# Four-ahead splits in an order that every engine keeps, and the loop over further blocks ahead of the experts

## The chip, the cores and the metric

The kernel runs on one core of a Trainium2 chip. The metric is the device time of one execution, in microseconds, as the median of several runs. Beside it there is one profiled execution with its own time; its span, from the first to the last instruction, is a little shorter than its time.

## What is computed

Two blocks of a sequence model stand one behind the other, on 1024 tokens of width 1024, all in fp32. The first has a gated convolution, a gated linear recurrence and a feed-forward layer, the second a state-space mixer, an mLSTM mixer and a mixture of experts. The change touches the mixture alone: 32 experts in 4 groups, each token goes to the two best experts of its best group.

```python
def hier_moe(h, wg, bg, we, be, w_gate, w_up, w_down):
    ...
    ids = (g_sel * EXPERTS_PER_GROUP + top_i).reshape(-1).astype(jnp.int32)
    order = jnp.argsort(ids)
    tok = order // TOP_K
    xs = xf[tok]
    sizes = jnp.bincount(ids, length=N_EXPERTS).astype(jnp.int32)
    hg = lax.ragged_dot(xs, w_gate.astype(xs.dtype), sizes)
    hu = lax.ragged_dot(xs, w_up.astype(xs.dtype), sizes)
    ys = lax.ragged_dot(jax.nn.silu(hg) * hu, w_down.astype(xs.dtype), sizes)
    ys = ys * gates.reshape(-1)[order][:, None].astype(ys.dtype)
    y = jax.ops.segment_sum(ys, tok, num_segments=t)
```

An expert's gate and up weights are 1024 x 512, its down weights 512 x 1024. 2048 rows are shared out over 32 experts, 64 on average.

## The kernel before, in words

The kernel has stages. `stage1`, `stage2` and `stage4` compute the first block, the mixers and, in `route` (L1462), the routing in two halves of 512 tokens. `stage5` (L1625) computes the experts, adds their two results to each token and normalises.

**Products.** Every fp32 product is made of three matmuls on a faster 32-bit type. `split` (L51) makes two tiles out of weights: ScalarE copies the high half (L56), VectorE, or GpSimd where `low` says so, subtracts it from the weights for the low half (L57). `mm3` (L84) issues high x high, high x low and low x high (L87 to L89). A pair of halves is a *unit*: 128 x 1024 weights, from a pool of five buffers. A unit feeds six matmuls of 128 x 512. `to_T` (L129) turns rows to columns on TensorE, four transposes per PSUM tile (L135), with a high half by ScalarE (L138) and a low half by VectorE out of PSUM (L139).

**The routing.** `route` computes each token's experts and its place within them, and makes with matmuls (L1589) the table `slots`: for the first 128 places of each expert the row of the result, the token and the gate. `sidx` (L1597) holds the first two as integers. Each half also scatters 16-byte records into a list in DRAM (`scatter`, 8 DMAs of GpSimd, L1611), which only the loop over further blocks reads. `cum` counts tokens per expert (L1593).

**The experts.** An expert has 12 units: four of the gate, four of up, four of down. The tokens of an expert are gathered by GpSimd's DMA into one of two tiles `xg` (L1654), transposed and split (`prep`), multiplied by gate and up (`wide`), `th = (tanh(gate/2) + 1) * gate` (L1713, L1714) and `th * up` (L1718), transposed and split again (`hidT`), multiplied by down (`down`), scaled by the gate (L1694) and scattered to `yd` (L1695). The Python loop runs expert e's gate, then the hidden transposes of e - 1, then expert e's up, the token transposes of e + 1 and the down of e - 1. Weights come as 1 MB tiles, two units each, on SP's queue, into 14 buffers (`rawt`).

What stands in the program is not the order on the engines: the framework's scheduler chooses, per engine, which ready instruction comes next, by its own estimate of times. Every sixth low half in the order of the calls is GpSimd's.

**Further blocks.** An expert with more than 128 tokens needs further blocks of 128. After e = 16 `overflow` (L1743) counts tokens with a matmul, makes a table of blocks `ti` with small jobs on VectorE (L1755 to L1773), loads the number of blocks into a register of every engine (L1774), and runs a loop with as many turns (L1776). With this data it has none: no instruction of its body is in the trace. Behind the loop a new block of the program begins.

Of the kernel before, what the change touches and what calls it, by code (L numbers as in the profile page):

```python
# [8 lines left out]
F32 = mybir.dt.float32  # L9
# [7 lines left out]
P = 128  # L17
S = 1024
# [13 lines left out]
class Net:  # L32
# [1429 lines left out]
    def route(self, hf, src, wk, small, wide, mx):  # L1462
# [106 lines left out]
        qs = []  # L1569
        for s, gt in ((0, pg), (1, m2)):  # L1570
# [21 lines left out]
        for tt in range(4):  # L1592
            v.tensor_tensor(self.cum, self.cum, OC[:, tt], ALU.add)  # L1593
# [29 lines left out]


    def stage5(self):  # L1625
        tc, nc, a = self.tc, self.nc, self.a
        self.wctx.close()
        with ExitStack() as ctx:
# [20 lines left out]
            def split(src, shape):  # L1649
                return self.split(src, shape, low=nc.gpsimd if self.nsplit % 6 == 5 else None)  # L1650

            def gather(e):
                x = xg[e % 2]
                nc.gpsimd.indirect_dma_start(  # L1654
                    out=x, out_offset=None, in_=self.h2d,
                    in_offset=bass.IndirectOffsetOnAxis(ap=self.sidx[:, 1, e:e + 1], axis=0),
                    bounds_check=S - 1, oob_is_err=False)

            def prep(e):
                xT = wk.tile([P, 2, KD, P], F32R, tag="xT5", name="xT5")  # L1660
                self.to_T(psa, xg[e % 2], (xT[:, 0], xT[:, 1]), 0)
                return xT

            def wide(w, e, xT):
                ps = psa.tile([P, DE], F32, tag="gu", name="gu", bufs=4)
                for k in range(0, KD, 4):
                    raw = self.rawt([P, 4, DE])
                    nc.sync.dma_start(raw, w[e, k * P:(k + 4) * P, :].rearrange("(k p) c -> p k c", p=P))
                    for j in range(0, 4, 2):
                        u = split(raw[:, j:j + 2], [2, DE])  # L1670
                        for i in range(2):
                            kk = k + j + i
                            self.mm3(ps, (xT[:, 0, kk], xT[:, 1, kk]), (u[0][:, i], u[1][:, i]), kk == 0, kk == KD - 1)
                return ps

            def hidT(hid):
                hT = wk.tile([P, 2, 4, P], F32R, tag="hT5", name="hT5")
                self.to_T(psa, hid, (hT[:, 0], hT[:, 1]), 0, nk=4)
                return hT

            def down(e, hT):
                pd = [psa.tile([P, 512], F32, tag="dn", name="dn") for _ in range(2)]
                for k in range(0, 4, 2):
                    raw = self.rawt([P, 2, D])
                    nc.sync.dma_start(raw, wd[e, k * P:(k + 2) * P, :].rearrange("(k p) c -> p k c", p=P))
                    for j in range(2):
                        u = split(raw[:, j], [D])
                        for ch in range(2):
                            s = slice(ch * 512, (ch + 1) * 512)
                            self.mm3(pd[ch], (hT[:, 0, k + j], hT[:, 1, k + j]), (u[0][:, s], u[1][:, s]), k + j == 0, k + j == 3)  # L1690
                y = wk.tile([P, D], F32, tag="y5", name="y5")
                gt = self.slots[:, 2, e:e + 1]
                for ch in range(2):
                    nc.scalar.activation(y[:, ch * 512:(ch + 1) * 512], pd[ch], AF.Copy, scale=gt)  # L1694
                i = nc.gpsimd.indirect_dma_start(  # L1695
                    out=self.yd, out_offset=bass.IndirectOffsetOnAxis(ap=self.sidx[:, 0, e:e + 1], axis=0),
                    in_=y, in_offset=None, bounds_check=2 * S - 1, oob_is_err=False)
                for o in self.ysc:
                    tc.declare_no_dep(i.ins, o.ins, reason="different rows")
                self.ysc.append(i)  # L1700

            self.ysc = []
            gather(0)
            gather(1)
            xT = prep(0)
            prev = None
            for e in range(NX + 1):
                if e < NX:
                    if e + 2 < NX:
                        gather(e + 2)  # L1710
                    pg = wide(wg, e, xT)
                    th = wk.tile([P, DE], F32, tag="th5", name="th5")
                    nc.scalar.activation(th, pg, AF.Tanh, scale=0.5)  # L1713
                    nc.vector.scalar_tensor_tensor(th, th, 1.0, pg, op0=ALU.add, op1=ALU.mult)  # L1714
                hT = hidT(prev) if e else None
                if e < NX:
                    pu = wide(wu, e, xT)
                    nc.vector.tensor_tensor(th, th, pu, ALU.mult)  # L1718
                    nxt = prep(e + 1) if e + 1 < NX else None
                if e:  # L1720
                    down(e - 1, hT)
                if e == 2:
                    self.scatter()
                if e == NX // 2:

                    self.overflow(mid, wk, psa, xg[(e + 1) % 2])
                prev, xT = th, nxt
# [15 lines left out]
    def overflow(self, mid, wk, psa, x):  # L1743
# [157 lines left out]
```

## Time and profile before

| | us |
|---|---|
| median of 3 runs | 3355.78 (3353.23 to 3355.95) |
| the profiled execution's own time | 3356.34 |
| its span | 3354.6 |
| TensorE matmuls busy | 3178.5 (95%) |
| TensorE weight loads busy | 2608.5 (78%) |
| VectorE busy | 2221.8 (66%) |
| ScalarE busy | 1520.8 (45%) |
| GpSimd busy | 825.0 (25%) |

The shares are means over all stages. The experts run from about 2680 to 3303 us, and in them the shares are others; so the profile is read there, by windows and by each engine's instructions in order of time. A matmul's duration reaches over the start of the next one; what counts is the distance from start to start. In a row of the timeline the number in brackets is the time the engine was idle just before, and what ended it.

### The profile page before, as it was taken

What the parts mean: (1) busy time and instruction counts of PE and PEld (TensorE: products, weight loads), DVE (VectorE), ACT (ScalarE), POOL (GpSimd) and SP (SyncE); (2) the same over time, 40 slices, a digit from 0 to 9 for tenths busy, and PEclk for the clock granted to TensorE, in tenths of its full rate; (3) what the DMA queues carried; (4) which work ended last, traced back from release to release, by engine and by line L of the source; (5) the groups of instructions that cost most, each with busy time, mean ns of one, the idle gap of its engine ahead of it and who ended that gap; (6) DMA issues with size and microseconds to landing.
All of it is one profiled execution on the core that took longest, in us unless ns stands there. A gap on an engine that the chain in (4) does not pass through costs nothing. (4 is left out here: it accounts for less than half of the span.)

```text
span 3354.6 us, 39834 instructions
## 1 busy us (share of the span) xinstructions
PE 3178.5 (95%) x15193; PEld 2608.5 (78%) x15193; DVE 2221.8 (66%) x2928; ACT 1520.8 (45%) x2069; POOL 825.0 (25%) x758
## 2 busy tenths in 40 slices
PE   8999999999999999999999999899999799989993
PEld 6887888877878888788777888777888677777772
DVE  5437545356475555455796656877657699999986
ACT  3327433246242222344443333433343278878773
POOL 0002210001253443000132111132112244434433
PEclk9999999999999999999999999999999899999997
DMA  4322444323422222555522323333332799969994
GB/s 156 100 89 91 142 155 145 126 92 113 169 76 91 76 79 91 199 193 202 159 88 88 107 82 102 96 116 109 121 101 83 265 340 371 370 241 391 374 357 162
DMA packets 347645, 546.04 MB, mean 163 GB/s; under 512 B 30320, under 2 KB 213116, under 8 KB 345660
## 3 DMA queue, kind: packets, MB, share of 16 engines
q1 hardware_dynamic: 307932, 470.01, 40.8%
q0 software_dynamic: 18640, 48.82, 4.0%
q10 hardware_dynamic: 20880, 24.65, 2.1%
q8 instruction: 120, 1.97, 0.2%
q14 instruction: 73, 0.60, 0.1%
HBM read 506.02 MB, written 54.17 MB: 167 GB/s over the span
## 5 line engine op out<-in xcount | busy, mean ns | idle before, releaser
L57 DVE TENSOR_TENSOR unit<-raw,unit 128x1024 fp32r<-128x1024 f32 x726 | 989.9, 1384 | 490.2 <-ACT unit L56 486.3
L56 ACT ACTIVATE unit<-raw 128x1024 fp32r<-128x1024 f32 (+1 forms) x790 | 813.7, 1045 | 749.9 <-PE acc L89 524.7
L87 PE MATMUL acc<-xT,unit 128*128 128x512 f32 x1360 | 542.8, 400 | 0.6 <-ACT xT L138 0.6
L88 PE MATMUL acc<-xT,unit 128*128 128x512 f32 x1360 | 536.0, 394 | 0.0
L89 PE MATMUL acc<-xT,unit 128*128 128x512 f32 x1360 | 534.3, 393 | 0.0
L87 PEld LDWEIGHTS acc<-xT,unit 128*128 128x128 f32 x1360 | 257.9, 190 | 55.1 <-issue 1.0
L88 PEld LDWEIGHTS acc<-xT,unit 128*128 128x128 f32 x1360 | 257.5, 189 | 54.3 <-issue 3.3
L89 PEld LDWEIGHTS acc<-xT,unit 128*128 128x128 f32 x1360 | 257.3, 189 | 54.0 <-issue 1.0
L57 POOL TENSOR_TENSOR unit<-raw,unit 128x1024 fp32r<-128x1024 f32 x64 | 176.5, 2758 | 273.6 <-issue 221.0
L88 PE MATMUL gu<-unit,xT 128*128 128x512 f32 x512 | 208.4, 407 | 17.4 <-DVE unit L57 12.4
L87 PE MATMUL gu<-unit,xT 128*128 128x512 f32 x512 | 206.1, 402 | 0.8 <-ACT xT L138 0.8
L89 PE MATMUL gu<-unit,xT 128*128 128x512 f32 x512 | 203.3, 397 | 0.1
L88 PE MATMUL acc<-unit,xT 128*128 128x256 f32 (+1 forms) x640 | 196.8, 307 | 2.0 <-DVE unit L57 2.0
L87 PE MATMUL acc<-unit,xT 128*128 128x256 f32 (+1 forms) x640 | 194.3, 309 | 2.6 <-ACT xb L1065 2.5
L89 PE MATMUL acc<-unit,xT 128*128 128x256 f32 (+1 forms) x640 | 196.0, 306 | 0.0
L88 PEld LDWEIGHTS gu<-unit,xT 128*128 128x128 f32 x512 | 96.9, 189 | 55.2 <-DVE unit L57 27.3
L87 PE MATMUL acc<-unit,hid 128*128 128x512 f32 x352 | 137.6, 391 | 0.0
L89 PE MATMUL acc<-unit,hid 128*128 128x512 f32 x352 | 137.2, 390 | 0.0
L88 PE MATMUL acc<-unit,hid 128*128 128x512 f32 x352 | 137.2, 390 | 0.0
L87 PEld LDWEIGHTS acc<-unit,xT 128*128 128x128 f32 x640 | 122.1, 191 | 11.1 <-ACT xb L1065 4.7
L642 PE MATMUL acc<-xe,unit 128*128 128x512 f32 x504 | 123.7, 396 | 5.9 <-DVE u L644 5.9
L88 PEld LDWEIGHTS acc<-unit,xT 128*128 128x128 f32 x640 | 122.3, 191 | 8.2 <-DVE unit L57 2.5
(485 smaller groups left out, 6332.3 us busy)
## 6 DMA issues: line engine op xcount, KB each, us to landing
raw<-in_w_in_dram SPq DMA_DIRECT2D x104, 1024.0 KB, 5.1
raw<-in_exp_w_gate_dram SPq DMA_DIRECT2D x64, 1024.0 KB, 9.6
raw<-in_exp_w_up_dram SPq DMA_DIRECT2D x64, 1024.0 KB, 9.6
raw<-in_exp_w_down_dram SPq DMA_DIRECT2D x64, 1024.0 KB, 10.1
raw<-in_w_ffn_down_dram SPq DMA_DIRECT2D x33, 1024.0 KB, 5.1
raw<-in_w_ffn_gate_dram SPq DMA_DIRECT2D x11, 1024.0 KB, 5.8
raw<-in_w_ffn_up_dram SPq DMA_DIRECT2D x11, 1024.0 KB, 5.1
hidD<-th ACTq DMA_DIRECT2D x44, 256.0 KB, 3.7
```

The source lines that it names most:

```text
L56: nc.scalar.activation(h, src, AF.Copy)
L57: (low or nc.vector).tensor_tensor(l, src, h.bitcast(F32), ALU.subtract)
L87: mm(out, w[0], x[0], start=first, stop=False)
L88: mm(out, w[0], x[1], start=False, stop=False)
L89: mm(out, w[1], x[0], start=False, stop=last)
L642: nc.tensor.matmul(ps, w[i], v[j], start=False, stop=(k == 3 and i == 1), skip_group_check=True)
```

## The change

The routing's second half makes the table of blocks (`blocks`), from the counts, ahead of the list of slots. `stage5` issues the loads of the first 16 units, memsets and the first two gathers, then the loop over further blocks. The list's second scatter has moved into the loop's body. Behind the loop the experts are one stream of units: gate, up of e, down of e - 1. While unit n is multiplied, unit n + 4 is split and the load for n + 16 is issued. GpSimd has the low half of a gate's and a down's first unit. Work of VectorE that follows a product stands one unit later (`later`). `in_order` ties each instruction of TensorE, ScalarE, VectorE and GpSimd behind the loop to the one ahead of it in the program, so that the scheduler has no choice there.

```diff
+        if hf:
+            for tt in range(4):
+                v.tensor_tensor(self.cum, self.cum, OC[:, tt], ALU.add)
+            self.blocks(wk, mx, ones)
         for s, gt in ((0, pg), (1, m2)):
...
+    def in_order(self, begin):
+        last = {}
+        for i in self.nc.cur_bb.bb.instructions[begin:]:
+            if i.engine not in (mybir.EngineType.PE, mybir.EngineType.Activation, mybir.EngineType.DVE, mybir.EngineType.Pool):
+                continue
+            if i.engine in last:
+                self.tc.add_manual_dep(
+                    i, last[i.engine].name,
+                    mybir.DependencyInfo(mybir.DependencyClass.NoSync, mybir.DependencyReason.DATA), reason="order")
+            last[i.engine] = i
...
-            def split(src, shape):
-                return self.split(src, shape, low=nc.gpsimd if self.nsplit % 6 == 5 else None)
...
+            stream = []
+            for e in range(NX + 1):
+                if e < NX:
+                    stream += [(e, 0, i) for i in range(4)] + [(e, 1, i) for i in range(4)]
+                if e:
+                    stream += [(e - 1, 2, i) for i in range(4)]
...
+            def split(n):
+                e, m, i = stream[n]
...
+                units[n] = self.split(src, [2, DE] if m < 2 else [D], low=nc.gpsimd if i == 0 and m != 1 else None)
+            AHEAD = 16
+            for n in range(AHEAD):
+                load(n)
             gather(0)
             gather(1)
...
+            self.overflow(wk, psa, mid.tile([P, D], F32, tag="gB", name="xo"))
+            self.nraw = AHEAD // 2
+            begin = len(nc.cur_bb.bb.instructions)
+            LEAD = 4
...
+            for n in range(LEAD):
+                split(n)
+            xT = x_T(0)
...
+            for n, (e, m, i) in enumerate(stream):
+                if n + AHEAD < len(stream):
+                    load(n + AHEAD)
+                if n + LEAD < len(stream):
+                    split(n + LEAD)
...
+                if m < 2:
+                    for k in range(2):
+                        kk = 2 * i + k
+                        self.mm3(pu if m else pg, (xT[:, 0, kk], xT[:, 1, kk]), (u[0][:, k], u[1][:, k]), kk == 0, kk == KD - 1)
...
+                for f in later.pop(n, ()):
+                    f()
+                if i < 3:
+                    continue
+                if m == 0:
                     nc.scalar.activation(th, pg, AF.Tanh, scale=0.5)
+                    if e:
+                        hT = wk.tile([P, 2, 4, P], F32R, tag="hT5", name="hT5")
+                        ps = tr(hid, 4, 0)
+                        high(hT, ps, 0)
+                    def one(th=th, pg=pg, hT=hT, ps=ps, e=e):
+                        nc.vector.scalar_tensor_tensor(th, th, 1.0, pg, op0=ALU.add, op1=ALU.mult)
+                        if e:
+                            low(hT, ps, 0)
+                    later[n + 1] = [one]
+                elif m == 1:
+                    hid = th
...
+                        for q in (0, 4):
+                            ps = tr(xg[(e + 1) % 2], KD, q)
+                            high(xT, ps, q)
+                            two.append((ps, q))
+                    def one(th=th, pu=pu, xT=xT, two=two):
+                        nc.vector.tensor_tensor(th, th, pu, ALU.mult)
+                        for ps, q in two:
+                            low(xT, ps, q)
+                    if 0 < e < NX - 1:
+                        later[n + 1] = [one]
+                    else:
+                        one()
...
+            self.in_order(begin)
...
         with tc.For_i(0, nb) as i:
+            self.scatter()
+            nc.gpsimd.memset(x, 0.0)
```

How it moves instructions is shown at three places. The first is VectorE in the middle of the experts. L57 is a low half of weights, `xT` and `hT` the low halves of tokens and of the hidden layer, `th` the products out of PSUM. Before:

```order
L1714 SCALAR_TENSOR_TENSOR th_20385<-th_20385,gu 128x512
L139 TENSOR_TENSOR hT_20388<-tp,hT_20388 128x512
L57 TENSOR_TENSOR unit<-raw,unit 128x1024 x3
L1718 TENSOR_TENSOR th_20385<-th_20385,gu 128x512
L57 TENSOR_TENSOR unit<-raw,unit 128x1024
L139 TENSOR_TENSOR xT_20438<-tp,xT_20438 128x512 x2
L57 TENSOR_TENSOR unit<-raw,unit 128x1024 x6
L1714 SCALAR_TENSOR_TENSOR th_20545<-th_20545,gu 128x512
```

Now, with L1780 for the first product, L1796 for the second and L1726 for the low halves out of PSUM:

```order
L1780 SCALAR_TENSOR_TENSOR th_20447<-th_20447,gu 128x512
L1726 TENSOR_TENSOR hT_20487<-tp,hT_20487 128x512
L57 TENSOR_TENSOR unit<-raw,unit 128x1024 x3
L1796 TENSOR_TENSOR th_20447<-th_20447,gu 128x512
L1726 TENSOR_TENSOR xT_20537<-tp,xT_20537 128x512 x2
L57 TENSOR_TENSOR unit<-raw,unit 128x1024 x7
L1780 SCALAR_TENSOR_TENSOR th_20607<-th_20607,gu 128x512
```

Of the seven low halves from the second product to the next expert's first one, one stood ahead of the tokens' low halves; now all seven stand behind them, and VectorE's three jobs out of PSUM follow each other. The second place is GpSimd in the same stretch: weights' low halves, gathers of tokens (`xg`) and scatters of results (`yd`). Before:

```order
L1654 DMA xg_19725<-h2d,sidx 128x1024
L57 TENSOR_TENSOR unit<-raw,unit 128x1024
L1695 DMA yd<-y_20167,sidx 2048x1024
L57 TENSOR_TENSOR unit<-raw,unit 128x1024
L1654 DMA xg_19724<-h2d,sidx 128x1024
L57 TENSOR_TENSOR unit<-raw,unit 128x1024
L1695 DMA yd<-y_20335,sidx 2048x1024
L57 TENSOR_TENSOR unit<-raw,unit 128x1024
```

Now:

```order
L57 TENSOR_TENSOR unit<-raw,unit 128x1024 x2
L1667 DMA xg_19749<-h2d,sidx 128x1024
L1810 DMA yd<-y_20435,sidx 2048x1024
L57 TENSOR_TENSOR unit<-raw,unit 128x1024 x2
L1667 DMA xg_19748<-h2d,sidx 128x1024
L1810 DMA yd<-y_20595,sidx 2048x1024
```

Before, a gather or a scatter stands between any two low halves; now the two low halves of an expert stand together, and gather and scatter behind them. The third place is GpSimd from the routing's end to the first expert. Before:

```order
L1611 DMA lst<-rec,row 32768x4
L1647 MEMSET xg_19724 128x1024
L1647 MEMSET xg_19725 128x1024
L1654 DMA xg_19724<-h2d,sidx 128x1024
L1654 DMA xg_19725<-h2d,sidx 128x1024
L1611 DMA lst<-rec,row 32768x4 x5
L1654 DMA xg_19724<-h2d,sidx 128x1024
L1611 DMA lst<-rec,row 32768x4 x2
L1750 MEMSET ov_22422 128x128
L1761 IOTA ov_i 128x16
L107 DMA gB<-in_norm_f_w_dram 128x1024
L57 TENSOR_TENSOR unit<-raw,unit 128x1024 x2
```

Now, from the last row of the loop's body, the branch back (L1875), on:

```order
L1875 UNCONDITIONAL_BRANCH
L1664 MEMSET xg_19748 128x1024
L1664 MEMSET xg_19749 128x1024
L1667 DMA xg_19748<-h2d,sidx 128x1024
L1667 DMA xg_19749<-h2d,sidx 128x1024
L57 TENSOR_TENSOR unit<-raw,unit 128x1024
L107 DMA gB<-in_norm_f_w_dram 128x1024
L1667 DMA xg_19748<-h2d,sidx 128x1024
L57 TENSOR_TENSOR unit<-raw,unit 128x1024
```

The list's eight scatters (`lst`) are gone from here, and the memsets and the first two gathers stand behind the loop, though the program's text has them ahead of it.

## Rows read from the trace of the kernel before

**Rows 1.** Windows: length; PE, PEld, DVE, ACT, POOL busy us; clock, DMA share, GB/s.

```profile
2720.00:2940.00 220.00, 215.04 (x988) 171.96 (x987) 215.92 (x178) 181.24 (x211) 97.62 (x47) 1.00 1.02 369
3020.00:3060.00 40.00, 39.16 (x180) 31.33 (x179) 39.24 (x33) 32.64 (x39) 18.56 (x9) 1.00 1.04 395
```

**Rows 2.** Timeline of ScalarE, Tanh and high half: start us, us, instruction, [idle].

```profile
2686.21 0.60 ACT L1713 ACTIVATE th<-gu 128x512 f32<-128x512 f32 x1 [0.34 <-PE gu L89]
2703.42 0.60 ACT L1713 ACTIVATE th<-gu 128x512 f32<-128x512 f32 x1 [0.34 <-PE gu L89]
2871.69 0.60 ACT L1713 ACTIVATE th<-gu 128x512 f32<-128x512 f32 x1 [0.34 <-PE gu L89]
2874.92 1.06 ACT L56 ACTIVATE unit<-raw 128x1024 fp32r<-128x1024 f32 x1 [0.25 <-PE gu L89]
2890.47 0.60 ACT L1713 ACTIVATE th<-gu 128x512 f32<-128x512 f32 x1 [0.33 <-PE gu L89]
3013.50 0.59 ACT L1713 ACTIVATE th<-gu 128x512 f32<-128x512 f32 x1
3031.59 0.60 ACT L1713 ACTIVATE th<-gu 128x512 f32<-128x512 f32 x1 [0.34 <-PE gu L89]
3242.90 0.60 ACT L1713 ACTIVATE th<-gu 128x512 f32<-128x512 f32 x1 [2.00 <-PE gu L89]
3283.33 0.60 ACT L1713 ACTIVATE th<-gu 128x512 f32<-128x512 f32 x1 [2.40 <-PE gu L89]
```

**Rows 3.** Timeline of TensorE, a steady expert: the wait, the token transposes.

```profile
2868.01 0.40 PE L87 MATMUL gu<-unit,xT 128*128 128x512 f32 x1
2868.82 0.50 PE L88 MATMUL gu<-unit,xT 128*128 128x512 f32 x1 [0.41 <-DVE unit L57]
...
2877.52 1.03 PE L135 MATMUL tp<-ident,xg 128*128 128x128 f32 x8
2878.31 0.48 PE L87 MATMUL dn<-unit,hT 128*128 128x512 f32 x1
```

**Rows 4.** Timeline of VectorE and GpSimd, one of the last experts.

```profile
3224.00 3.50 DVE L57 TENSOR_TENSOR unit<-raw,unit 128x1024 fp32r<-128x1024 f32 x3 [0.26 <-ACT unit L56]
3228.14 0.69 DVE L1718 TENSOR_TENSOR th<-th,gu 128x512 f32<-128x512 f32 x1 [0.65 <-PE gu L89]
...
3226.94 2.82 POOL L57 TENSOR_TENSOR unit<-raw,unit 128x1024 fp32r<-128x1024 f32 x1 [4.07 <-issue]
```

**Rows 5.** Timeline of GpSimd and VectorE, a steady expert.

```profile
2856.02 3.10 POOL L57 TENSOR_TENSOR unit<-raw,unit 128x1024 fp32r<-128x1024 f32 x1 [5.15 <-issue]
2865.21 2.47 POOL L57 TENSOR_TENSOR unit<-raw,unit 128x1024 fp32r<-128x1024 f32 x1 [4.11 <-issue]
...
2857.23 4.11 DVE L57 TENSOR_TENSOR unit<-raw,unit 128x1024 fp32r<-128x1024 f32 x2 [0.37 <-ACT unit L56]
2864.19 9.11 DVE L57 TENSOR_TENSOR unit<-raw,unit 128x1024 fp32r<-128x1024 f32 x6
```

**Rows 6.** Timeline of VectorE, GpSimd and TensorE at the start of the experts.

```profile
2670.14 0.26 DVE L1594 TENSOR_TENSOR slots<-slots,mx 128x96 f32<-128x96 f32 x1 [2.55 <-PE mx L1589]
...
2668.81 1.86 POOL L1647 MEMSET xg<- 128x1024 f32 x2
2671.53 1.17 POOL L1654 DMA_INDIRECT xg<-h2d,sidx  x1 [0.85 <-POOL xg L1647]
...
2687.43 2.39 POOL L57 TENSOR_TENSOR unit<-raw,unit 128x1024 fp32r<-128x1024 f32 x1
...
2677.46 1.97 PE L135 MATMUL tp<-ident,xg 128*128 128x128 f32 x8 [7.36 <-DMA xg<-h2d,sidx]
```

**Rows 7.** Timeline of VectorE and GpSimd at the loop over further blocks.

```profile
2997.02 0.19 DVE L1755 COPY ov_n<-cnt 128x32 f32<-128x32 f32 x1 [2.40 <-PE cnt L1752]
3002.47 0.18 DVE L1772 CAST ov_t<-ov_f 128x32 int32<-128x32 f32 x1
...
3004.46 1.03 POOL L1654 DMA_INDIRECT xg<-h2d,sidx  x1 [5.61 <-issue]
```

More of the change, by code (lines that the diff above doesn't have):

```diff
@@ L1591, in route @@
                 n += 1
-        for tt in range(4):
-            v.tensor_tensor(self.cum, self.cum, OC[:, tt], ALU.add)
+        if not hf:
+            for tt in range(4):
+                v.tensor_tensor(self.cum, self.cum, OC[:, tt], ALU.add)
         v.tensor_tensor(self.slots, self.slots, pl[:, 0:3 * NX].rearrange("p (j e) -> p j e", e=NX), ALU.add)
@@ L1657, in gather @@
                     bounds_check=S - 1, oob_is_err=False)
[L1659 to L1666, printed above, removed]
-                    raw = self.rawt([P, 4, DE])
[L1668 to L1683, printed above, removed]
-                    raw = self.rawt([P, 2, D])
[L1685 to L1700, printed above, removed]
@@ L1703, in stage5 @@
+            def split(n):
+                e, m, i = stream[n]
+                raw = rawd[e, m, i // 2 * 2]
+                src = raw[:, i % 2 * 2:i % 2 * 2 + 2] if m < 2 else raw[:, i % 2]
+                units[n] = self.split(src, [2, DE] if m < 2 else [D], low=nc.gpsimd if i == 0 and m != 1 else None)
+            AHEAD = 16
+            for n in range(AHEAD):
+                load(n)
             gather(0)
             gather(1)
[L1705 to L1708, printed above, removed]
+            self.ysc = []
@@ new lines, in stage5, with tr, high @@
+            self.overflow(wk, psa, mid.tile([P, D], F32, tag="gB", name="xo"))
+            self.nraw = AHEAD // 2
+            begin = len(nc.cur_bb.bb.instructions)
+            LEAD = 4
+            later = {}
+            def tr(xn, nk, k0):
+                ps = psa.tile([P, 4, P], F32, tag="tp", name="tp")
+                for j in range(4):
+                    nc.tensor.transpose(ps[:, j], xn[:, (k0 + j) * P:(k0 + j + 1) * P], self.ident)
+                return ps
+            def high(dst, ps, k0):
+                nc.scalar.activation(dst[:, 0, k0:k0 + 4], ps, AF.Copy)
@@ L1709, in stage5 @@
+            for n, (e, m, i) in enumerate(stream):
[3 more added lines that the diff above has]
+                    split(n + LEAD)
+                u = units.pop(n)
+                todo = []
+                if m == 0 and i == 0:
                     if e + 2 < NX:
                         gather(e + 2)
-                    pg = wide(wg, e, xT)
+                    pg = psa.tile([P, DE], F32, tag="gu", name="gu", bufs=4)
@@ L1722, in stage5 @@
[L1722 to L1727, printed above, removed]
+                elif m == 1 and i == 0:
+                    pu = psa.tile([P, DE], F32, tag="gu", name="gu", bufs=4)
+                elif m == 2 and i == 0:
+                    pd = [psa.tile([P, 512], F32, tag="dn", name="dn") for _ in range(2)]
+                    if e == NX - 1:
+                        hT = wk.tile([P, 2, 4, P], F32R, tag="hT5", name="hT5")
+                        ps = tr(hid, 4, 0)
+                        high(hT, ps, 0)
+                        low(hT, ps, 0)
@@ new lines, in stage5 @@
+                if m < 2:
+                    for k in range(2):
+                        kk = 2 * i + k
+                        self.mm3(pu if m else pg, (xT[:, 0, kk], xT[:, 1, kk]), (u[0][:, k], u[1][:, k]), kk == 0, kk == KD - 1)
+                else:
+                    for ch in range(2):
+                        s = slice(ch * 512, (ch + 1) * 512)
+                        self.mm3(pd[ch], (hT[:, 0, i], hT[:, 1, i]), (u[0][:, s], u[1][:, s]), i == 0, i == 3)
+                for f in later.pop(n, ()):
+                    f()
```

95 lines of the change are left out of this document (64 added, 31 removed).

## The prediction, written before the changed kernel had run

> **What bounds the kernel now.** Begin with the windows [rows 1]. In the 220 us of the first row VectorE is busy 215.9, TensorE's matmuls 215.0, ScalarE 181.2, GpSimd 97.6: two engines look full. The Tanh of each expert comes once per expert, so the starts of two of them give the period: 2890.47 - 2871.69 = 18.78 us [rows 2]. The same view has one period of 18.09 (3013.50 to 3031.59), just after the loop over further blocks, when VectorE had no backlog; and over the last two experts it has (3283.33 - 3242.90) / 2 = 20.2. The 31 periods from 2686.21 to 3283.33 are the place where this change acts; what stands before the routing keeps its order.
>
> Who waits in a period of 18.78? TensorE, once: a matmul starts 0.81 us after the one ahead of it, 0.41 of it idle for a low half of VectorE [rows 3]. Take the 18.09 for TensorE without waits: eight transposes and their restart are 0.9 (2877.52 to 2878.31 and 0.1), four of them 0.4, which leaves (18.1 - 1.3) / 72 = 0.233 from matmul to matmul. The wait is then 0.81 - 0.23 = 0.58 and a slower restart 0.1, and 18.1 + 0.7 = 18.8 closes the account: TensorE alone would take 18.1 per expert. So VectorE sets the 18.78. Of a period it is busy 215.9 / 220 x 18.78 = 18.4 us. Ten low halves, at 1.15 (three take 3.50), and five half-sized jobs out of PSUM, at up to 0.69 [rows 4], are 14.4 of these. The other 4.0 are in [rows 5]: six halves take 9.11 instead of 6.9, two take 4.11 instead of 2.3, each time across one low half on GpSimd (2.47 and 3.10 us, at 2865.21 and 2856.02). A job of VectorE with both operands in SBUF stands while GpSimd's runs; 2.2 and 1.8 are lost, and 0.37 is idle just ahead of the second.
>
> A job that reads PSUM does not stand. In [rows 4] GpSimd works from 3226.94 for 2.82 us, and in the middle of it VectorE's product with the up projection takes its plain 0.69. All depends on what VectorE has to do while GpSimd splits.
>
> **The change, part by part.** *Order.* Low halves on GpSimd stay two per expert, but are now those of a gate's and a down's first unit, and the order is fixed. I walk one expert, with zero where the gate's last matmul is issued. A unit is six matmuls, 1.40. TensorE: four transposes 0.4, up to 6.0, eight transposes 0.9, down 6.9 to 12.5, next gate 12.5 to 18.1. ScalarE, whose high halves (1.06, [rows 2]) take a unit's buffer when TensorE leaves it: Tanh and hidden high half to 1.3, high half of down's first unit to 2.3; after down's start that of the next gate's first unit to 8.8. GpSimd therefore splits from 2.3 to 4.7 and from 8.8 to 11.2. VectorE: gate product and hidden low half 1.2 to 2.6, both from PSUM, then blocked until 4.7; three halves to 8.1; up product and two token low halves (PSUM) to 9.9 (0.6 each, back to back), blocked until 11.2; seven halves to 19.5, which is 1.4 into the next expert, where it began at 1.2. It does not fall further behind, because the next block ends at 4.7 again. TensorE needs the tightest of these (next gate's first unit, 11.2) at 12.7 and the second (12.3) at 14.1: margins of 1.5 and 1.8. So TensorE never waits, and its 18.1 is the period. From the second Tanh (2703.42) to the last (3283.33) now pass 579.9 us; 30 x 18.1 = 543.0. **-36.9.** The stop for the loop in the middle and the slow last experts are inside this.
>
> The Trainium skill would read [rows 1] otherwise: its page "Perfetto Trace Analysis", section "Identifying the Most-Contended Engine", takes VectorE's occupancy as a fair measure of how full it is, and TensorE's by weight loads. By that VectorE, 98% busy, stays the bound, since it loses no job here, and the sum would be that of the first rival. But by [rows 5], 4 us of that occupancy are standing.
>
> *First experts.* From the first Tanh to the second is 17.21. TensorE waits there for a GpSimd half that starts only at 2687.43 [rows 6], behind the eight list scatters, which now run only inside the loop body and, with no further block, never. Eight units are 11.2, eight transposes 0.8 (2877.52 to 2878.31, [rows 3]) and 0.1 of restart; the first gate of the second expert has no down ahead to hide its token halves, 0.9. Together 13.0. **-4.2.**
>
> *Start.* It pays. (1) The table's VectorE jobs took 5.6 us (2997.02 to 3002.65, [rows 7]); of the 19 now, 12 stand ahead of the gather index, by their share 3.6 us, and between routing jobs, whose latency they fill, they cost less. Bounds 0 (VectorE idles there 2.55 us for TensorE's matmuls, [rows 6]) and 3.6; I take 1.9, about half, since those ahead of these matmuls delay them and those behind fill the wait. The index, 0.3 behind the first row of [rows 6], comes at 2672.3 instead of 2670.4. (2) The other seven are 2.1 us by their share, with two routing jobs and the index 2.6: 2674.9. (3) All engines read the count and branch: GpSimd went on at 3004.46, 1.8 after the last table entry (3002.47 + 0.18): 2676.7. (4) The two memsets and gathers, ahead of the branch in the text, stand behind it in GpSimd's order: memsets 1.86, 0.3, and from gather to the first transpose 5.93 (2671.53 to 2677.46): 2684.8 instead of 2677.46. **+7.3**, between +3 and +11. First units are split meanwhile: four high halves and GpSimd's 2.4 behind two gathers end about when the tokens have been transposed. Eight loads are issued ahead of the branch, six more at once behind it; the eight cover sixteen units, over 22 us.
>
> *At nothing:* the twelve last units behind the last Tanh (as many as before), the final norm (order unchanged), and the loads: per expert 369 GB/s x 18.78 = 6.93 MB, over 18.1 us 383 GB/s, and 395 were moved from 3020 to 3060 [rows 1]. Should the transfers stay at 369, each expert is 0.7 us short, 21 us or seven tiles over all, of fourteen buffers.
>
> Sum: -36.9 - 4.2 + 7.3 = -33.8. The profiled execution took 3356.34 (its span 3354.6 and 1.7 around), 0.6 above the median of 3355.78. 3356.3 - 33.8 - 0.6 = 3322; I say **3322**.
>
> **Rivals.** *VectorE stays the bound* (GpSimd's halves slip to where VectorE splits too): the period stays 18.78, 30 x 0.68 = 20.4 more, **3342**. For it: the standing of [rows 5], and any lag that shifts the pairs. Against: the walk returns to itself, and it would have to lag by over 1.5. Chance 0.15.
>
> *Slower: four units are too short a lead.* ScalarE now cannot pass a Tanh or PSUM copy that waits for TensorE, and GpSimd's half hangs behind it. If the next gate's first low half ends over 1.5 us later than in the walk, TensorE stops in every expert. Its price in the trace is what order alone did to the last experts, 20.2: 30 x 2.1 = 63 more, **3385**. It turns slower than before at a period of 18.1 + 33.8 / 30 = 19.2. For it: 20.2 was seen with no lack of work; GpSimd's half has taken 3.10. Against: even that leaves 0.8. Chance 0.09.
>
> *It does half of what it says:* the stop in the middle goes, but the period stays 18.78 as in the first rival, the first experts do not gain their 4.2, since their halves queue as before, and the start is at its bound, 3.7 more: 20.4 + 4.2 + 3.7 = 28.3 more, **3350**, within 0.2%. For it: the first gather now waits for the branch, and its pieces come from another place of the program. Against: the list scatters are out of GpSimd's way in any case. Chance 0.07.
>
> **How the numbers follow.** Forecast 0.69: 3322, with +-5 from the start and +-6 from 0.2 us of period: 3311 to 3333. The range 3311 to 3344 takes in the first rival. A measurement of this kernel tells 0.2%, 6.7 us. Faster, under 3349: forecast and first rival, 0.84. Same, the third: 0.07. Slower, over 3362.5, the second: 0.09.
>
> **What would show it.** Tanh to Tanh 18.1, without a gap in the middle and at the end; TensorE without waits for low halves; GpSimd's halves beside VectorE's PSUM jobs; VectorE's busy share below 98%; first token transposes near 2685; no list scatter after the routing's first half. Wrong if the period stays at 18.8 with VectorE full (first rival), if TensorE waits for GpSimd in each expert (second), or if ScalarE waits for weights.

## The result: 0.87% faster, and the profile after

The changed kernel took 3326.43 us (median of 4 runs, 3324.03 to 3327.16), the kernel before beside it 3355.86 (4 runs, 3353.23 to 3356.15): a ratio of 0.9913, 95% interval 0.9901 to 0.9925. 3322 was forecast, the range was 3311 to 3344. The profiled execution took 3324.03, its span went from 3354.6 to 3322.3 us.

First the windows of the changed kernel, with the columns of [rows 1]:

```profile
2720.00:2940.00 220.00, 220.00 (x1021) 179.25 (x1020) 209.21 (x183) 187.38 (x221) 101.57 (x50) 1.00 1.02 379
3020.00:3060.00 40.00, 40.00 (x190) 32.71 (x189) 38.20 (x34) 33.46 (x41) 16.92 (x9) 1.00 1.03 378
3060.00:3220.00 160.00, 160.00 (x741) 130.29 (x740) 151.91 (x133) 136.25 (x160) 74.53 (x36) 1.00 1.01 368
```

In these windows TensorE is busy in every microsecond; VectorE has gone from 98% to 95%. Next its Tanhs on ScalarE's timeline, which answer to [rows 2]:

```profile
2693.74 0.60 ACT L1773 ACTIVATE th<-gu 128x512 f32<-128x512 f32 x1 [0.34 <-PE gu L89]
2707.83 0.60 ACT L1773 ACTIVATE th<-gu 128x512 f32<-128x512 f32 x1 [0.34 <-PE gu L89]
...
2870.86 0.60 ACT L1773 ACTIVATE th<-gu 128x512 f32<-128x512 f32 x1 [0.34 <-PE gu L89]
2888.98 0.60 ACT L1773 ACTIVATE th<-gu 128x512 f32<-128x512 f32 x1 [0.34 <-PE gu L89]
...
3251.24 0.60 ACT L1773 ACTIVATE th<-gu 128x512 f32<-128x512 f32 x1 [0.34 <-PE gu L89]
```

The first is 7.5 us later than before. From the first to the second are 14.09 us, and the 30 periods behind them are 18.11 or 18.12 each, with no stop in the middle and no slow end: 543.41 us instead of 579.9. From the last Tanh to the end of the span are 71.06 us, before 71.27.

One steady expert on the timelines of VectorE and GpSimd, which answer to [rows 5]:

```profile
2871.70 0.68 DVE L1780 SCALAR_TENSOR_TENSOR th<-th,gu 128x512 f32<-128x512 f32 x1
2872.30 0.68 DVE L1726 TENSOR_TENSOR hT<-tp,hT 128x512 fp32r<-128x512 f32 x1
2873.88 4.92 DVE L57 TENSOR_TENSOR unit<-raw,unit 128x1024 fp32r<-128x1024 f32 x3 [0.90 <-ACT unit L56]
2878.72 0.68 DVE L1796 TENSOR_TENSOR th<-th,gu 128x512 f32<-128x512 f32 x1
2879.32 1.27 DVE L1726 TENSOR_TENSOR xT<-tp,xT 128x512 fp32r<-128x512 f32 x2
2880.52 9.37 DVE L57 TENSOR_TENSOR unit<-raw,unit 128x1024 fp32r<-128x1024 f32 x7
...
2873.04 2.40 POOL L57 TENSOR_TENSOR unit<-raw,unit 128x1024 fp32r<-128x1024 f32 x1 [5.04 <-ACT unit L56]
2879.44 2.43 POOL L57 TENSOR_TENSOR unit<-raw,unit 128x1024 fp32r<-128x1024 f32 x1 [4.00 <-ACT unit L56]
```

The tokens' two low halves, out of PSUM, run beside GpSimd's second half and keep their 0.6 us each (1.27 for both); the product and the hidden low half end just before its first half begins, the second product just before its second. Each of GpSimd's halves outlasts these jobs: three halves of VectorE take 4.92 instead of 3.50 ([rows 4]), seven take 9.37 instead of about 8.1. So VectorE still stands (is busy without getting on) for 2.7 us per expert instead of 4.0.

The start, on the timelines of VectorE, GpSimd and TensorE, which answers to [rows 6]:

```profile
2670.96 0.18 DVE L1602 TENSOR_SCALAR sidx<-slots 128x64 int32<-128x64 f32 x1
2673.09 0.17 DVE L1864 CAST ov_t<-ovw 128x16 int32<-128x16 f32 x1
...
2674.36 1.84 POOL L1664 MEMSET xg<- 128x1024 f32 x2 [16.64 <-DVEq L1875]
2676.37 2.13 POOL L1667 DMA_INDIRECT xg<-h2d,sidx  x1 [0.17 <-POOL xg L1664]
...
2684.29 1.97 PE L1719 MATMUL tp<-ident,xg 128*128 128x128 f32 x8 [14.13 <-DMA xg<-h2d,sidx]
```

### The profile page after: what moved, and what is told of

It is laid out like the page before. It is cut to its first block, busy times and chain, and to the rows that moved or that the text cites. A ratio compares the mean times of both kernels' runs of the same rounds, so it can differ in the third digit from the quotient of the medians.

```text
span 3322.3 us, 39873 instructions
## 1 busy us (share of the span) xinstructions
PE 3157.1 (95%) x15193; PEld 2605.7 (78%) x15193; DVE 2195.9 (66%) x2929; ACT 1522.2 (46%) x2069; POOL 811.4 (24%) x749
## 5 line engine op out<-in xcount | busy, mean ns | idle before, releaser
L57 DVE TENSOR_TENSOR unit<-raw,unit 128x1024 fp32r<-128x1024 f32 x726 | 962.7, 1349 | 489.8 <-ACT unit L56 488.7
L57 POOL TENSOR_TENSOR unit<-raw,unit 128x1024 fp32r<-128x1024 f32 x64 | 154.9, 2420 | 290.0 <-ACT unit L56 249.6
L87 PEld LDWEIGHTS acc<-unit,xT 128*128 128x128 f32 x640 | 121.6, 190 | 11.0 <-ACT xb L1065 4.7
L88 PEld LDWEIGHTS acc<-unit,xT 128*128 128x128 f32 x640 | 121.7, 190 | 8.2 <-DVE unit L57 2.5
L89 PEld LDWEIGHTS acc<-unit,xT 128*128 128x128 f32 x640 | 121.8, 190 | 5.4 <-issue 0.2
## 6 DMA issues: line engine op xcount, KB each, us to landing
raw<-in_exp_w_gate_dram SPq DMA_DIRECT2D x64, 1024.0 KB, 16.8
raw<-in_exp_w_up_dram SPq DMA_DIRECT2D x64, 1024.0 KB, 15.4
```

What stands on the lines that cost most here:

```text
L57: (low or nc.vector).tensor_tensor(l, src, h.bitcast(F32), ALU.subtract)
L87: mm(out, w[0], x[0], start=first, stop=False)
L88: mm(out, w[0], x[1], start=False, stop=False)
L89: mm(out, w[1], x[0], start=False, stop=last)
```

## The experiments

All ratios are to the kernel before on the same chip, with their 95% intervals. The distances are those from Tanh to Tanh, worked out from rows like those above; "start" is from the index `sidx` to the first Tanh.

| kernel | ratio | start | first to second | period after that |
|---|---|---|---|---|
| before | 1 | 15.8 | 17.21 | 18.78; one of 29.1; last five 19.5 to 21.4 |
| changed | 0.9913 (0.9901 to 0.9925) | 22.8 | 14.09 | 18.11 |
| changed, once more | 0.9915 (0.9899 to 0.9932) | 21.6 | 14.08 | 18.11 |
| GpSimd at the third unit | 0.9976 (0.9966 to 0.9986) | 22.3 | 16.10 | 18.68 |
| no halves on GpSimd | 0.9905 (0.9888 to 0.9921) | 21.6 | 13.50 | 18.11 |
| before, no halves on GpSimd | 0.9913 (0.9896 to 0.9929) | 15.4 | 14.34 | 18.11; one of 28.3; last five 18.5 to 19.6 |
| before, loop moved alone | 1.0058 (1.0041 to 1.0075) | 23.3 | 16.96 | 18.78; 19.2 to 23.9 from the 16th to the 18th expert; then 20.5 (last 19.9) |
| the same, no halves on GpSimd | 0.9958 (0.9941 to 0.9974) | 23.6 | 13.40 | 18.11; from the 17th on 19.3 to 19.6 (last 19.0) |
| changed, order not kept | 1.0033 (1.0019 to 1.0047) | 23.0 | 16.77 | 18.11; from the 22nd on 22.0 to 22.6 (last 21.6) |
| lead of three | 0.9910 (0.9893 to 0.9926) | 21.6 | 13.98 | 18.11 |
| first gather ahead | 0.9917 (0.9900 to 0.9934) | 25.3 | 14.09 | 18.11 |
| that, no halves on GpSimd | 0.9902 (0.9886 to 0.9919) | 21.6 | 13.50 | 18.11 |
| loop at the end | 0.9854 (0.9838 to 0.9870) | 14.4 | 13.39 | 17.71 |
| tiles shifted by 64 bytes | 0.9890 (0.9873 to 0.9906) | 21.9 | 15.57 | 17.71 |

The theory at the outset: VectorE stands beside GpSimd's halves, and where these are placed decides the period. Rival A: the kept order and the lead of four do it.

**GpSimd's halves moved by two units.**

```diff
-low=nc.gpsimd if i == 0 and m != 1 else None
+low=nc.gpsimd if i == 2 and m != 1 else None
```

> The changed kernel, but GpSimd has the low half of a gate's and a down's third unit instead of the first; everything else, the fixed order and the lead of four too, stays. Theory: VectorE's low halves stand while GpSimd's runs and its jobs out of PSUM don't, so the place of GpSimd's halves decides. There they meet VectorE's run of low halves: two times about 2.1 us of standing instead of the 2.7 in all now, VectorE needs 18.5 to 19.2 us per expert and sets the period; 30 periods of it make the time 3338 to 3358. Rival A: the order that every engine keeps and the lead of four are what helped; then the period stays 18.1 and the time 3326. In the trace: six or three halves of VectorE over 1.2 us each wherever GpSimd splits, and TensorE idle for VectorE's halves (theory), or TensorE full (rival).

The period is 18.68, the time 3350.52: the theory. The expert on the timelines of VectorE, GpSimd and TensorE:

```profile
2905.47 5.69 DVE L57 TENSOR_TENSOR unit<-raw,unit 128x1024 fp32r<-128x1024 f32 x3
2911.08 0.68 DVE L1796 TENSOR_TENSOR th<-th,gu 128x512 f32<-128x512 f32 x1
2912.88 8.22 DVE L57 TENSOR_TENSOR unit<-raw,unit 128x1024 fp32r<-128x1024 f32 x6
...
2905.51 3.43 POOL L57 TENSOR_TENSOR unit<-raw,unit 128x1024 fp32r<-128x1024 f32 x1 [5.62 <-issue]
2911.92 2.41 POOL L57 TENSOR_TENSOR unit<-raw,unit 128x1024 fp32r<-128x1024 f32 x1 [2.98 <-ACT unit L56]
...
2896.80 0.50 PE L88 MATMUL gu<-unit,xT 128*128 128x512 f32 x1 [0.30 <-DVE unit L57]
```

The first half begins with VectorE's run of three (2.2 us of standing), the second behind the product (1.3), and once per expert TensorE waits for VectorE again, as in [rows 3].

**No half on GpSimd.** `low=None` in the changed kernel, and in the kernel before:

```diff
-                return self.split(src, shape, low=nc.gpsimd if self.nsplit % 6 == 5 else None)
+                return self.split(src, shape, low=None)
```

> The changed kernel, but GpSimd has no low half at all; VectorE makes all twelve of an expert. Theory: VectorE then has 12 x 1.14 + 5 x about 0.65 = 16.9 us of work per expert and nothing stands, so it stays under TensorE's 18.1: the period stays 18.1, VectorE's busy share in the middle falls or stays (93 to 95%, with all the work on it), and the time is 3323 to 3327, a little less because the first to the second Tanh shortens from 14.1 towards 13.0. Rival: VectorE's busy share of 95% is real work; two halves more, 2.3 us, make it the bound at 19.4, 30 x 1.3 = 39 us more, 3365.

> The kernel before, its order, scheduler and loop untouched, but GpSimd has no low half: VectorE makes all twelve of an expert. Theory (VectorE's standing beside GpSimd's halves is what held the period at 18.78; new order, lead and loop are not needed for that): nothing stands, VectorE needs about 16.9 us per expert, TensorE sets 18.1 in the middle too. Up to the loop some 14 periods lose 0.67 us each and behind it about ten, 16 us; the stop in the middle (11 us) and the last experts at 20 stay: 3356 - 16 = 3340, 3334 to 3344. Rival A (the order and the lead of four are what gives 18.1): the period stays 18.78 or grows towards 19.5, since VectorE gets two halves more: 3356 to 3378.

Both as the theory had it, the second by more. VectorE makes all twelve halves, and TensorE is full, in the windows of the changed kernel so edited and of the kernel before so edited:

```profile
2720.00:2940.00 220.00, 220.00 (x1022) 179.32 (x1021) 203.55 (x207) 187.55 (x220) 34.59 (x25) 1.00 1.02 382
```

```profile
2720.00:2940.00 220.00, 220.00 (x1022) 179.00 (x1021) 206.82 (x208) 187.99 (x218) 24.34 (x24) 1.00 1.03 384
```

With two halves more to do, VectorE is busy for 203.6 and 206.8 us instead of 209.2 and 215.9: GpSimd's help cost VectorE more than it saved. On the timeline of the first of them seven halves take 8.03 us:

```profile
2869.77 8.03 DVE L57 TENSOR_TENSOR unit<-raw,unit 128x1024 fp32r<-128x1024 f32 x7
```

So the new order was not needed for the period. Where the kernel before gains: its 31 distances sum to 571.59 us instead of 597.12, its 28.3 us stop included.

**The loop alone, and the order not kept.** First, the loop, its table and the list's second scatter ahead of the kernel before's experts:

```diff
+            self.overflow(wk, psa, mid.tile([P, D], F32, tag="gB", name="xo"))
             xT = prep(0)
...
-                if e == 2:
-                    self.scatter()
-                if e == NX // 2:
-
-                    self.overflow(mid, wk, psa, xg[(e + 1) % 2])
```

> The kernel before with one part of the change alone: the table of blocks in the routing, the loop over further blocks and the list's second scatter ahead of the experts. Order, lead and GpSimd's halves are as before. Theory: the start is later as in the changed kernel, first transposes 2684 to 2686 (+7 to +8); the stop in the middle, 13 to 14 us of the 16.5 by which 579.9 exceeds 30 x 18.78, is gone; the period stays 18.8. Sum -6, 3347 to 3352. Rival B: the loop in the middle spoiled the order around it and the period falls to 18.1 over the whole length when it is gone, 3328 to 3332.

Both theories fail: 18 us slower than before. The start pays the 7.5 us, the one long distance in the middle (29.1) is gone, but from the 19th expert on the period is 20.5, that of the kernel before's last experts: the scheduler falls into another order and stays in it. In the traces VectorE's order there is the same as in the kernel before's 29th and 30th expert, and the passage from one order to the other costs a distance of 23.9. In the kernel before, the loop in the middle renewed the order: from the 19th to the 24th expert it is again that of the experts ahead of the loop. The same with all halves on VectorE:

> The kernel before with the loop and its table ahead of the experts (as in the experiment with the loop alone) and all twelve low halves on VectorE; the scheduler chooses the order. Theory: nothing stands, so as long as the scheduler keeps the order of the first experts the period is 18.1; where it falls into the order of the last ones (the loop alone had 20.5 from the 18th on) it is 19.3, as the last experts of the kernel before with all halves on VectorE had. So the order costs 14 x 1.2 = 17 us once the loop no longer renews it, and the start 7.5: 3340 to 3348. Rival: 20.5 was VectorE's standing too, and without it the period is 18.1 over the whole length: 3326.

As the theory had it: 19.33 from the 19th expert on. By these two kernels, 1.2 of the 2.4 us between 18.11 and 20.5 come with the order and 1.2 with GpSimd's halves. This split is an estimate, since the two late orders are not the same on TensorE. And the changed kernel without `self.in_order(begin)`:

> The changed kernel without the ties that keep each engine's order: the scheduler chooses again among ready instructions, with the same units on GpSimd and the same lead of four in the text. Theory (it is the meeting of GpSimd's halves with VectorE's that sets the period): as long as the order stays near the text's, 18.1 to 18.3 per expert, with single periods up to 18.8 where it departs (late experts), 3326 to 3336. Rival A (the kept order is the gain): the period goes back to 18.8 as before, 30 x 0.67 = 20 us more, 3346.

Slower than both theories said, 3369.80 us where the kernel before took 3358.51. One of the late experts on the timelines of TensorE, VectorE and GpSimd:

```profile
3107.16 0.50 PE L88 MATMUL gu<-unit,xT 128*128 128x512 f32 x1 [0.41 <-DVE unit L57]
3110.50 0.50 PE L88 MATMUL gu<-unit,xT 128*128 128x512 f32 x1 [1.68 <-DVE unit L57]
3117.20 0.50 PE L88 MATMUL dn<-unit,hT 128*128 128x512 f32 x1 [0.61 <-DVE unit L57]
...
3105.89 5.68 DVE L57 TENSOR_TENSOR unit<-raw,unit 128x1024 fp32r<-128x1024 f32 x3
3112.57 5.70 DVE L57 TENSOR_TENSOR unit<-raw,unit 128x1024 fp32r<-128x1024 f32 x3
...
3106.94 2.42 POOL L57 TENSOR_TENSOR unit<-raw,unit 128x1024 fp32r<-128x1024 f32 x1 [4.87 <-ACT unit L56]
3113.12 2.94 POOL L57 TENSOR_TENSOR unit<-raw,unit 128x1024 fp32r<-128x1024 f32 x1 [3.75 <-ACT unit L56]
```

Both of GpSimd's halves fall on VectorE's runs of halves, and TensorE waits four times in the expert: the three rows and a shorter wait of 0.15 at 3103.70. Kept order is what lets the loop leave the middle: it holds for the 32 experts what the scheduler holds for some fifteen to twenty.

**A lead of three** (`LEAD = 3`):

> The changed kernel with a lead of three units instead of four (the order is kept, so ScalarE's high half of a unit now stands one unit later against Tanh and the copies out of PSUM). Theory: my walk leaves margins of 1.5 and 1.8 us and a unit is 1.40, so a lead of three is just still enough or short by a few tenths: period 18.1 to 18.4, time 3326 to 3336 beside the changed kernel's 3326. Rival C (the lead itself is the lever): the period goes to 19 or more, over 3350. If the buffers, not the text's lead, decide, it is 18.11 exactly and the same time.

18.11 and the same time, as the expectation's last sentence has it: the lead in the text has room to spare.

**The first gather ahead of the loop**, tied ahead of GpSimd's reading of the count:

```diff
+            first = len(nc.cur_bb.bb.instructions)
             gather(0)
+            self.ysc = []
+            self.overflow(wk, psa, mid.tile([P, D], F32, tag="gB", name="xo"), first)
             gather(1)
-            self.ysc = []
-            self.overflow(wk, psa, mid.tile([P, D], F32, tag="gB", name="xo"))
...
+        self.in_order(first, (mybir.EngineType.Pool,))
```

> The changed kernel with both memsets and the first gather ahead of the loop on GpSimd, tied ahead of its reading of the count; the second gather behind the loop. Theory (the place of the gather sets the start): gather at about 0.3 behind the index instead of 5.4, first transposes 6 to 8 us after it, as the lines of the two kernels show, so 3 to 5.4 us earlier than in the changed kernel: time 3321 to 3324 beside its 3326. Rival D (weights or branch decide: the six loads issued behind the branch slow the rows down, or the first units are late): transposes at most 2 us earlier, no difference that shows.

> The first gather ahead of the loop and no low half on GpSimd, together. Theory: the two gains lie in different places (first transposes; first to second Tanh 14.1 to 13.5) and add up: 3 to 5.4 and 0.6 us less than the changed kernel, 3320 to 3323, the period 18.11. Rival: what holds the first expert once the rows are earlier is the split of its first units; then nothing is gained over the gather alone.

No gain from the gather. The timeline of the first of the two (VectorE, GpSimd, SP's queue, ScalarE), and below it a window with the columns of [rows 1]:

```profile
2678.10 0.18 DVE L1865 CAST ov_t<-ovw 128x16 int32<-128x16 f32 x1
...
2676.97 1.09 POOL L1667 DMA_INDIRECT xg<-h2d,sidx  x1 [5.21 <-DVE ovw L1860]
...
2684.31 0.90 SPq L1691 DMA_DIRECT2D raw<-in_exp_w_down_dram  x2
2684.48 3.90 ACT L56 ACTIVATE unit<-raw 128x1024 fp32r<-128x1024 f32 x4 [18.28 <-issue]
...
2681.00:2682.00 1.00, 0.00 (x0) 0.00 (x0) 0.00 (x0) 0.00 (x0) 0.00 (x0) 0.50 0.00 0
```

SP and ScalarE go on 6.0 and 6.2 us after the table's last entry, where it was 1.0 in the changed kernel (GpSimd 1.1). The gather's bytes have moved by 2681; GpSimd's queue waits until 2681.37 and then takes 1.7 us for a step at the loop's boundary (`INC_SWDGE_SEM` in the trace) that in the changed kernel ran while the table was still being made; the engines' queues go on from 2683.4. So the boundary waits until the gather on its way is done. The first transposes come 4.3 us earlier after the index (9.0 instead of 13.3), but the four high halves that lay under the gather now lie behind it, ahead of the tokens' high half in the kept order. And VectorE's first low halves now meet GpSimd's (VectorE, GpSimd, TensorE):

```profile
2686.51 6.15 DVE L57 TENSOR_TENSOR unit<-raw,unit 128x1024 fp32r<-128x1024 f32 x3 [8.24 <-ACT unit L56]
...
2686.93 2.37 POOL L57 TENSOR_TENSOR unit<-raw,unit 128x1024 fp32r<-128x1024 f32 x1
...
2693.32 0.80 PE L89 MATMUL gu<-unit,xT 128*128 128x512 f32 x1 [3.17 <-DVE xT L1727]
```

Three halves take 6.15 us instead of 3.50, and TensorE waits 3.17 us for the tokens' low halves behind them. The first Tanh comes 2.6 us later after the index than in the changed kernel. In the combination, without halves on GpSimd, this wait is 0.72 and the first Tanh is back at 21.6, that of no halves on GpSimd alone. So neither expectation of the combination came: against its theory the gather adds nothing (0.9902 beside 0.9905), and against its rival it is 3.7 us better at the start than the gather alone.

**The loop behind the last expert**, with no halves on GpSimd:

```diff
-            self.overflow(wk, psa, mid.tile([P, D], F32, tag="gB", name="xo"))
...
+                x4 = raws[0].tile([P, 2, D], F32, tag="raw", name="x4")
...
+            self.rawt = lambda shape, name="raw": raws[3].tile(shape, F32, tag="raw", name=name)
+            self.overflow(wk, psa, xg[0])
```

> The changed kernel once more, unaltered, beside the next two on the same chip: 0.9913 of the kernel before, as at first.

> The changed kernel without GpSimd's low halves, and with the loop over further blocks behind the last expert instead of ahead of the first (its table stays in the routing, the order is kept; the last residual rows are loaded ahead of the loop, the body borrows a gather buffer and two weight buffers). Theory: the branch and the gather's place behind it are what the start pays, about 7 us from the index to the first Tanh (22.8 against 15.8 before); that goes, and at the end the branch costs 1 to 3 us, because the engines wait there for the last scatter in any case: 3 to 6 us less than the changed kernel, 3319 to 3323 in its terms, 0.989 to 0.990 of the kernel before. Rival: the loop's boundary waits for every transfer that is out (the residual rows too) and the norm's transfers start later by 8 us or more: no gain or a loss.

3308.52 us beside 3328.12 for the changed kernel, 19.6 less: the best of all. The theory had 3 to 6. From the index to the first Tanh 7.3 are gained, from the first to the second 0.7 (0.6 is that of no halves on GpSimd), and 2.2 of them are given back at the end (from the last scatter to the first load behind it 5.6 us instead of 3.3): 5.8, as the theory had it. Another 12.0 come from where nobody looked: TensorE's period is 17.71 instead of 18.11, 30 times. The last 1.8 were not traced; the four times of a kernel lie up to 4.6 apart. In the middle of an expert, TensorE's timeline of the changed kernel, run once more, and of this one:

```profile
2901.06 0.40 PE L89 MATMUL dn<-unit,hT 128*128 128x512 f32 x1
2901.29 0.39 PE L87 MATMUL dn<-unit,hT 128*128 128x512 f32 x1
2901.53 0.40 PE L88 MATMUL dn<-unit,hT 128*128 128x512 f32 x1
```

```profile
2901.12 0.39 PE L87 MATMUL gu<-unit,xT 128*128 128x512 f32 x1
2901.34 0.39 PE L88 MATMUL gu<-unit,xT 128*128 128x512 f32 x1
2901.57 0.39 PE L89 MATMUL gu<-unit,xT 128*128 128x512 f32 x1
```

On average from 2720 to 2940 us a matmul follows the one ahead by 0.233 us there and 0.2275 here (from start to start within a product, without pairs that miss a record between them), at a granted clock of 1.00 in both, with the same instructions in the same order on TensorE. What differs for its operands is addresses: a tile of 64 bytes that only the loop's body uses is no longer placed ahead of the transposed tiles.

**The shift alone.** The changed kernel with the body's small tile put elsewhere; its order is that of the changed kernel on every engine:

```diff
-            rc = wk.tile([P, 4], I32, tag="ov_r", name="ov_r")
+            rc = wk.tile([P, DE], F32, tag="th5", name="ov_r")[:, 0:4].bitcast(I32)
```

The built program's addresses, in bytes within a partition (the first buffer of each):

```
             xT5     mod 128    hT5     mod 128
before      174944      96     195424      96
changed     171872      96     192352      96
loop at end 171808      32     192288      32
shifted     175904      32     192288      32
```

> The changed kernel, every instruction and its order on every engine unaltered; only the small tile of the loop's body (64 bytes of each partition, ahead of the tokens' and the hidden layer's transposed tiles) now shares the buffers of the products, so that xT5 and hT5, TensorE's stationary operands in the experts, start at an address with remainder 32 of 128 instead of 96, as they do in the experiment with the loop at the end. Theory (the start address of the stationary operand sets how fast one matmul follows the next; it is why that experiment had 0.229 us from matmul to matmul and a period of 17.71 instead of 0.2345 and 18.11): the period becomes 17.7, 31 x 0.4 = 12.4 us less than the changed kernel, about 0.9878 of the kernel before. Rival (the place of the loop, or of the experts' code behind or ahead of a loop, does it): the period stays 18.11 and the time is the changed kernel's, 0.9913.

The Tanhs of two successive experts and the window:

```profile
2870.99 0.60 ACT L1773 ACTIVATE th<-gu 128x512 f32<-128x512 f32 x1 [0.30 <-PE gu L89]
2888.70 0.60 ACT L1773 ACTIVATE th<-gu 128x512 f32<-128x512 f32 x1 [0.30 <-PE gu L89]
...
2720.00:2940.00 220.00, 220.00 (x1042) 183.00 (x1041) 211.25 (x188) 191.23 (x224) 106.48 (x51) 1.00 1.02 381
```

17.71 again, and 0.9890 of the kernel before. The addresses do it, and the place of the loop does not. The time falls by less than the 12.4 us expected, by 7.7 as the ratios have it: 12.0 are gained in the 30 periods, but its first to second Tanh is 1.5 longer (15.57), and the end behind the last Tanh at least as much (72.7 instead of 71.0 to 71.3). In both places it is mostly TensorE's clock. A window of the first, behind a wait of TensorE of 1.38 us:

```profile
2704.60:2708.40 3.80, 3.76 (x10) 2.94 (x11) 2.43 (x3) 1.06 (x1) 0.00 (x0) 0.55 1.04 394
```

Most matmuls follow each other there by 0.43 us, the pace at the lower of the clock's two levels, 1.2 GHz. The changed kernel, run once more, had a wait of 1.22 at this place, and a granted clock of 1.00 behind it. Three other kernels have such a stretch between their first two Tanhs: halves at the third unit, loop moved alone, and order not kept. `th5` and `y5` moved too; which tile it is, and which remainders are good, was not separated.

## Why the prediction was right, and where it was not

**The periods (-36.9, measured -36.5).** The walk held: VectorE loses 2.3 and 1.3 us per expert across GpSimd's halves (idle time and standing), 2.1 and 1.3 in the walk, and TensorE waits for none. That VectorE stood in the old order is shown by the halves moved by two units and by the kernels without them; that its jobs out of PSUM don't stand, by the tokens' low halves that keep their length beside GpSimd's second half, and by [rows 4]. The Trainium skill says the same of the ports ("SBUF — State Buffer", section "Who interferes with whom": a VectorE instruction with two SBUF inputs contends with a GpSimd instruction that reads SBUF, one with at most one, outside VectorE's 2-port modes, does not), and these rows agree. The Trainium skill's reading by occupancy ("Perfetto Trace Analysis", section "Identifying the Most-Contended Engine") would have had VectorE as the bound; the kernels in which VectorE got more work and was less busy (203.6 and 206.8 us of 220) show that 98% was partly waiting.

What the walk missed is that nothing had to be arranged. It took GpSimd's two halves for needed help. VectorE alone needs 16.9 us per expert (203.6 / 220 x 18.11 = 16.8 measured), and an edit of one line in the kernel before reaches the same 0.9913. And its floor is none: "TensorE alone would take 18.1 per expert" holds for one placement of tiles, and for another it is 17.71.

**The first experts (-4.2, measured -3.1).** 13.0 was forecast, 14.09 measured. The missed 1.1 lies where TensorE waits for the second expert's token halves, which come in VectorE's order behind a product and three halves that GpSimd blocks (4.87 us for 3.50). On TensorE's timeline:

```profile
2702.39 0.50 PE L89 MATMUL gu<-unit,xT 128*128 128x512 f32 x1 [1.22 <-DVE xT L1726]
```

Without GpSimd's halves the wait is 0.64 and the distance 13.50, so they are 0.6 of it. The other 0.5 stays without them: the forecast's 0.9 for the token halves was too little. It was not taken apart further.

**The start (+7.3 to the first transposes, measured +6.8; to the first Tanh +7.5).** Right by errors that cancel. The index came 0.5 us later, not 1.9: the table's jobs filled VectorE's wait for TensorE. The rest of the table took 2.3, not 2.6. GpSimd went on 1.1 after the last entry, not 1.8, at 2674.36 instead of 2676.7. From there to the gather it was 2.0, not 2.2. But from gather to transposes it was 7.92 instead of 5.93, 2.0 more. The issue alone holds GpSimd for 2.13 us instead of 1.17 ([rows 6]), which may be half of it. Why is open: four loads are issued in the 2.2 us before it and two more beside it, but before, too, the queues moved 390 GB/s during a gather of 5.93; and in the experiment with the gather ahead, alone on the queues, its last byte had moved 4 us after its issue. That the loads slow it was not tried by itself. From the transposes to the first Tanh it was another 0.7 more than before, which the forecast did not have; part of it is the clock (last section).

**The end, the norm and the loads** cost nothing, as forecast: 368 to 379 GB/s were enough, though less than the 383 worked out for this period.

**Sum.** -36.5 - 3.1 + 7.5 - 0.2 = -32.3, against -33.8: the profiled execution came out 1.5 above its forecast. The median of 3326.43 is 4.4 above 3322: beside these 1.5, the profiled execution is 2.4 under the median of its runs, where the forecast took it to be 0.6 above, as before.

**The rivals.** VectorE as the bound, the short lead and the half effect did not come. The price put on the second, 20.2 for "what order alone did to the last experts", was mixed: with all halves on VectorE the last experts took 19.3, so by this estimate order is 1.2 of it and GpSimd's halves the rest; and in these kernels the order failed only where nothing renewed it.

## What to carry to other kernels

Before work is shared out to GpSimd, take it away from it once: a helper that reads SBUF can make VectorE stand for longer than it helps. A busy share near 100% beside such a helper is to be split into working and standing, by the length of the same job with and without the helper, before it is called a bound. And where an engine seems to run at its own pace, compare that pace between kernels with the same instructions: here start addresses that differ by 64 bytes in their remainder were worth 0.4 us of every period, 12 us in all, more than the loop's place (7.3 - 2.2 = 5.1).

## What was not expected of the hardware

- 128x512 matmuls follow each other by 0.2275 or 0.233 us at the same clock, with the tiles' addresses as the only difference found.
- A loop that turns no time still waits at its boundary for a gather on its way: 6.2 us instead of 1.0 from the table's last entry until ScalarE goes on. With the loop behind the experts the boundary cost 2.2.
- The start varies between executions of the same kernel by the clock: after TensorE's wait of 14.13 us the granted clock was 0.70 in the first 10 us of the changed kernel's experts, and matmuls followed each other by 0.43 us until 2690.04; the second profiled execution had its 0.23 earlier, and its start was 1.1 us shorter. In the shifted kernel a window behind a wait of 1.38 us had 0.55.

```profile
2684.00:2694.00 10.00, 9.71 (x34) 7.84 (x35) 5.63 (x6) 5.58 (x7) 1.05 (x1) 0.70 1.03 383
```
